# The first feed-forward matrix by seven block products per pair of weight chunks, with half-width matmuls

## The chip, the cores and the metric

One core of one Trainium2 chip runs the whole program. The metric is the device time of one execution in microseconds, as the median over several executions; lower is better. The engines named below are TensorE (PE in the rows, its weight loads PEld), VectorE (DVE), ScalarE (ACT), GpSimd (POOL) and SyncE (SP, which here only starts transfers).

## The reference, cut to what matters

A one-layer decoder trunk on 512 tokens with model width 1024: a mixer (attention and a state-space branch, merged by gates and projected by `w_out`), and then a feed-forward block. All inputs are fp32. The change touches the end of it:

```
h = h + hybrid_mixer(rmsnorm(h, norm1_w), ...)       # its last step: merged @ w_out
gate, up = split(rmsnorm(h, norm2_w) @ w_ffn_in, 2)   # 1024 -> 2 x 2816
h = h + (silu(gate) * up) @ w_ffn_out                 # 2816 -> 1024
return rmsnorm(h, final_norm_w)
```

## The kernel before, in words

**Layout.** Activations lie transposed: 128 features on the partitions, 512 tokens along the row. Every weight matrix is cut into chunks of 128 output features by 1024 (or 512, 768) input features, 512 KB each, and a chunk lies as eight 128x128 tiles side by side.

**Precision.** An fp32 operand is split into a high part, rounded by a copy into the fp32r type, and a low part, the remainder. A product takes three matmuls per 128x128 tile: high times high, high times low, low times high. For weights, class `Weights` (L43) does it for one running list of all chunks: SP loads a raw chunk (L63, tile `wraw`), ScalarE copies the high part (L79, `whi`), VectorE subtracts it from the raw chunk for the low part (L80, `wlo`). It loads two chunks ahead of use and splits one ahead. `project` (L159) takes the next chunk and issues its 24 matmuls of 512 columns (line L104), in one PSUM bank, and at its middle and end runs functions that wait in the list `late` (the norm's steps, for example).

**The stages around the change.** The output projection (L839 to L857) runs eight `project` calls; each result is added to the residual x and gives one 128-feature block `h1` (L843). ScalarE and VectorE split it, scaled by `norm2_w`, into `h1h` and `h1l` (L848, L849), and its squares are summed over blocks by GpSimd (L857). The first feed-forward stage (L870 to L884) has 22 pairs of chunks, gate and up: 2 x 24 matmuls for each pair. The norm's factor per token, `rb2`, is worked out beside the first chunks (`second_norm`, L865) and is multiplied onto gate and up as they leave PSUM (L875, L879); then a tanh (L877), two products on VectorE (L880, L881), and the result `us` is split at once (L179, L180, tiles `hhh`, `hhl`). The second feed-forward stage (L886 to L899) runs, for each of seven output blocks, 22 tiles x 3 matmuls of 512 columns, adds to the residual (L891), squares and scales. The eighth block is written out by hand (`last_block`, L907, and `last_norm`, L919) in two halves of 256 tokens, so 66 matmuls of 256 columns for each half, and the final norm of the first half runs beside the second.

**What sets the order.** Outside the two sections ordered by hand (the start, and the eighth block), a planner orders the instructions of each engine: by their order in the program and by when it expects their inputs. Each engine then runs its list in order. Tiles are taken from pools with a fixed number of buffers per name; a new tile waits until the last reader of the one whose buffer it takes is done. SP, ACT and POOL each start transfers from their own list, so a start waits behind whatever stands before it there.

Of the kernel before, what the change touches and what calls it, by code (L numbers as in the profile page):

```python
# [14 lines left out]
P = 128  # L15
# [11 lines left out]
WARM = 10  # L27

# [63 lines left out]

@with_exitstack
def trunk(ctx: ExitStack, tc: tile.TileContext, xT, w_in, w_v, w_dt, w_attn, w_ssm, w_out, w_fi, w_fo,
# [37 lines left out]
    wst = Weights(nc, wp, _chunk_plan(w_in, w_v, w_attn, w_ssm, w_out, w_fi, w_fo))  # L132
# [26 lines left out]
    def project(ps, rhs, first=True, last=True, at=None):  # L159
        h, l, kt = wst.next()  # L160
# [89 lines left out]
    la_d = drm.tile([NSH, S], F32, name="la_d")  # L250
    v_d = [drm.tile([P, NCH, S], F32, name=f"v_d{g}") for g in range(2)]
# [583 lines left out]
    hp_ = ctx.enter_context(tc.tile_pool(name="h1", bufs=1, reuse_waits="tile", side="right"))  # L835
    h1, h1w = [], []
    h1a = hp_.tile([P, KD, S], F32, name="h1a")
    ssq = None
    for j in range(KD):  # L839
        t = h1a[:, j, :]  # L840
# [4 lines left out]
        h1.append(t)  # L845
        hi = hp_.tile([P, S], F32R, name=f"h1h{j}")
        lo = hp_.tile([P, S], F32R, name=f"h1l{j}")
        act.activation(hi, t, AF.Copy, scale=par("n2", j))  # L848
        ev.scalar_tensor_tensor(lo, t, par("n2", j), hi.bitcast(F32), op0=ALU.mult, op1=ALU.subtract)  # L849
        h1w.append((hi, lo))  # L850
        sq = hp_.tile([P, S], F32, tag="sq", name=f"sq2_{j}", bufs=2)
        act.activation(sq, t, AF.Square)
        if j == 0:
            ssq = hp_.tile([P, S], F32, tag="ssq", name="ssq2")
            gp.tensor_copy(ssq, sq)
        else:
            gp.tensor_add(ssq, ssq, sq)  # L857
    mg_cm.__exit__(None, None, None)
# [4 lines left out]
    rb2 = fp.tile([P, S], F32, name="rb2")  # L863

    def second_norm():  # L865
        r = mean_pow(fp, [ssq], D, EPS, "n2")
        late.append(lambda: act.activation(rb2, spread(r), AF.Copy))

    late.append(second_norm)
    pend = [project(bank("mm"), h1w), project(bank("mm"), h1w)]  # L870
    hh = []
    for j in range(NF):
        pg, pu = pend
        gs = fp.tile([P, S], F32, tag="gs", name=f"gs{j}", bufs=2)
        ev.tensor_mul(gs, pg, rb2)  # L875
        th = fp.tile([P, S], F32, tag="fth", name=f"fth{j}", bufs=2)
        act.activation(th, gs, AF.Tanh, scale=0.5)  # L877
        us = fp.tile([P, S], F32, tag="us", name=f"us{j}", bufs=2)
# [77 lines left out]
def _chunk_plan(w_in, w_v, w_attn, w_ssm, w_out, w_fi, w_fo):  # L956
# [16 lines left out]
    for j in range(NF):  # L973
        plan += [w_fi[j], w_fi[NF + j]]
# [87 lines left out]
```

## Time and profile before

| | us |
|---|---|
| median of 3 runs | 1175.6 (1175.52 to 1177.36) |
| the profiled execution | 1176.68 |
| its span, first to last instruction | 1174.8 |
| output projection | 755.55 to 799.12 |
| first feed-forward stage | 799.12 to 1042.21 |
| second feed-forward stage, blocks 0 to 6 | 1042.21 to 1147.95 |
| eighth block | 1147.95 to the end |

The bounds are the starts of the first matmuls with the stage's operands in the profile's timeline. Times in the rows count from the span's start. A matmul's duration in the rows holds its fill and drain, so neighbouring matmuls overlap; what one costs in a stream is the distance between two starts.

### The profile page before, as it was taken

How to read it: one execution, taken by the hardware profiler on the slowest of the kernel's cores; microseconds unless marked ns; L12 is line 12 of the kernel's file. 1: busy time of each engine (PE TensorE's matmuls, PEld its weight loads, DVE VectorE, ACT ScalarE, POOL GpSimd, SP SyncE). 2: the span in 40 equal slices, each digit the busy share in tenths (PEclk: the TensorE clock that was granted, in tenths of full speed). 3: DMA queues.
4: the chain of work that ended last, by engine and by line, in shares of the span. 5: the costliest groups of instructions: out<-in, count | busy, mean ns of one | idle time of the engine just before them, and what ended most of it. 6: DMA issues, size and time to landing. Idle time of an engine off the chain costs nothing.

```text
span 1174.8 us, 14966 instructions
## 1 busy us (share of the span) xinstructions
PE 1162.8 (99%) x5844; PEld 960.6 (82%) x5844; DVE 632.8 (54%) x1045; ACT 473.6 (40%) x822; POOL 156.3 (13%) x136
## 2 busy tenths in 40 slices
PE   9999999999999999999999999999999999999997
PEld 6777888878888988888888888888888888888886
DVE  5787898874577423456555434454554554532222
ACT  5555465553454321354654533343322322322221
POOL 2214313131112200010110100031000000000001
PEclk9999999999999999999999999999999999999999
DMA  5442323233222343232332213433223333233322
GB/s 211 138 156 92 107 90 116 100 115 102 90 88 75 127 161 106 90 91 82 83 75 88 64 64 99 172 120 93 90 90 108 90 91 107 90 86 94 99 81 72
DMA packets 40584, 120.20 MB, mean 102 GB/s; under 512 B 5368, under 2 KB 11024, under 8 KB 40129
## 3 DMA queue, kind: packets, MB, share of 16 engines
q1 hardware_dynamic: 38224, 116.71, 31.3%
q10 hardware_dynamic: 1296, 2.22, 0.5%
q0 software_dynamic: 992, 0.31, 0.3%
q8 instruction: 46, 0.75, 0.2%
q14 instruction: 26, 0.20, 0.1%
HBM read 114.88 MB, written 4.34 MB: 101 GB/s over the span
## 4 chain that ended last, share of the span: by engine, by line
PE 94%; DVE 2%; issue 1%; DMA 1%; ACT 1%; POOL 0%; SPq 0%; DVEq 0%; ACTq 0%; POOLq 0%
PE mm L104 85%; PE aux L104 7%; PE aux L107 2%; DVE xm L378 0%; DVE wlo L80 0%; DMA x<-xT 0%; DMA la_d<-laf 0%; DMA lab<-la_d 0%; DVE a L470 0%; DVE acc L442 0%; ACT whi L79 0%; ACT xnh L382 0%; DVE xul L301 0%; DVE h1a L941 0%; DVE a L472 0%
## 5 line engine op out<-in xcount | busy, mean ns | idle before, releaser
L79 ACT ACTIVATE whi<-wraw 128x1024 fp32r<-128x1024 f32 (+2 forms) x193 | 198.4, 1028 | 463.1 <-PE mm L104 358.7
L80 DVE TENSOR_TENSOR wlo<-wraw,whi 128x1024 fp32r<-128x1024 f32 (+2 forms) x193 | 238.8, 1238 | 221.8 <-ACT whi L79 221.8
L104 PE MATMUL mm<-xnh,wlo 128*128 128x512 f32 x640 | 254.6, 398 | 0.0
L104 PE MATMUL mm<-xnh,whi 128*128 128x512 f32 x640 | 253.1, 395 | 0.9 <-DVE acc L442 0.8
L104 PE MATMUL mm<-xnl,whi 128*128 128x512 f32 x640 | 252.4, 394 | 0.0
L104 PEld LDWEIGHTS mm<-xnh,wlo 128*128 128x128 f32 x640 | 120.4, 188 | 27.7 <-issue 2.7
L104 PEld LDWEIGHTS mm<-xnh,whi 128*128 128x128 f32 x640 | 120.4, 188 | 27.5 <-issue 1.6
L104 PEld LDWEIGHTS mm<-xnl,whi 128*128 128x128 f32 x640 | 120.3, 188 | 26.6 <-issue 1.2
L104 PE MATMUL mm<-h1h,wlo 128*128 128x512 f32 x352 | 138.8, 394 | 0.0
L104 PE MATMUL mm<-h1l,whi 128*128 128x512 f32 x352 | 138.0, 392 | 0.0
L104 PE MATMUL mm<-h1h,whi 128*128 128x512 f32 x352 | 136.7, 388 | 0.0
L104 PEld LDWEIGHTS mm<-h1l,whi 128*128 128x128 f32 x352 | 66.1, 188 | 15.4
L104 PEld LDWEIGHTS mm<-h1h,whi 128*128 128x128 f32 x352 | 66.1, 188 | 14.7
L104 PEld LDWEIGHTS mm<-h1h,wlo 128*128 128x128 f32 x352 | 66.2, 188 | 13.2
L104 PE MATMUL mm<-hhh,wlo 128*128 128x512 f32 (+1 forms) x198 | 72.9, 368 | 0.0
L104 PE MATMUL mm<-hhl,whi 128*128 128x512 f32 (+1 forms) x198 | 72.6, 367 | 0.0
L104 PE MATMUL mm<-hhh,whi 128*128 128x512 f32 (+1 forms) x198 | 72.4, 365 | 0.0
L442 DVE SCALAR_TENSOR_TENSOR acc<-mm,hcw,acc 128x511 f32<-128x511 f32 (+2 forms) x72 | 53.2, 743 | 1.2 <-ACT acc L440 0.2
L475 POOL TENSOR_TENSOR ce<-ce,Cf 128x768 f32<-128x768 f32 x16 | 34.8, 2177 | 139.4 <-ACT ce L474 78.6
L104 PE MATMUL mm<-ssmh,wlo 128*128 128x512 f32 x128 | 50.6, 395 | 0.0
L104 PE MATMUL mm<-ssml,whi 128*128 128x512 f32 x128 | 50.5, 395 | 0.0
L104 PE MATMUL mm<-ssmh,whi 128*128 128x512 f32 x128 | 49.8, 389 | 0.0
(256 smaller groups left out, 1646.6 us busy)
## 6 DMA issues: line engine op xcount, KB each, us to landing
wraw<-w_in SPq DMA_DIRECT2D x80, 512.0 KB, 3.5
wraw<-w_fi SPq DMA_DIRECT2D x44, 512.0 KB, 3.5
lab<-la_d SPq DMA_DIRECT2D x16, 512.0 KB, 3.7
wraw<-w_ssm SPq DMA_DIRECT2D x16, 512.0 KB, 3.6
wraw<-w_fo SPq DMA_DIRECT2D x16, 512.0 KB, 3.5
wraw<-w_v SPq DMA_DIRECT2D x11, 512.0 KB, 3.5
wraw<-w_out SPq DMA_DIRECT2D x8, 512.0 KB, 3.5
wraw<-w_fo SPq DMA_DIRECT2D x8, 384.0 KB, 3.1
```

Source lines behind the costliest of these rows:

```text
L79: self.nc.scalar.activation(hi[:, cs], r[:, cs], AF.Copy)
L80: self.nc.vector.tensor_sub(lo[:, cs], r[:, cs], hi[:, cs])
L104: pe.matmul(out, lhsT, rhs, start=start, stop=stop, skip_group_check=True)
L107: pe.transpose(out, src, ident)
L442: ev.scalar_tensor_tensor(acc[:, d:], ps[:, : S - d], hcw[:, t * 4 + 3 - d : t * 4 + 4 - d], acc[:, d:], op0=ALU.mult, op1=ALU.add)
L475: gp.tensor_mul(ce, ce, Cf[:, P:].unsqueeze(1).to_broadcast([P, 2, S - P]))
```

## The change

The first feed-forward stage no longer multiplies each chunk with all eight blocks of `h1`. A pair of chunks is seen as a 2x2 matrix of blocks (gate and up, by the first and the last four tiles), the normalised input as a 2x2 matrix too (first and last four feature blocks, by first and last 256 tokens). Their four result blocks come from seven block products instead of eight, over sums and differences of the blocks (Winograd's form of Strassen's scheme). Each product has 4 tiles x 3 matmuls of 256 columns.

- The right-hand sums are made once, in the output projection, whose blocks now come in the order 0, 4, 1, 5, 2, 6, 3, 7 (`OUT_ORDER`); the residual `h1` is written to DRAM there and read back for the second stage.
- For every pair, class `Pairs` loads both raw chunks; the four left-hand sums are added on VectorE and split as before; the three blocks used as they are (a11 and a12 in one piece, a22) get their low part otherwise: ScalarE writes the high part, then its negative into the low part's tile, and a transfer issued by GpSimd adds the raw weights from DRAM onto it.
- Partial sums are copied out of PSUM by ScalarE and added by VectorE. The factor `rb2` is multiplied onto the gate alone; for the up half it is multiplied in the second stage (`rb2h`).
- The first two `us` are split at once (`EARLY`), the other 20 after the stage. The second stage begins with blocks 0 and 1 in turn, eight tiles at a time.

```diff
+class Pairs:
+    def parts(self, pool, tag, name):
+        return tuple(pool.tile([P, KD * P], F32R, tag=tag % n, name=f"{name}_{n}", bufs=3) for n in ("hi", "lo"))
+    def load(self, n):
...
+        r1 = self.wp.tile([P, KD * P], F32, tag="wraw", name=f"fa{n}")
+        r2 = self.fw.tile([P, KD * P], F32, tag="wraw2", name=f"fb{n}", bufs=2)
+        for t, src in ((r2, b), (r1, a)):
+            self.nc.sync.dma_start(t.rearrange("p (k n) -> p k n", n=P), src)
+    def added(self, hi, lo, raw, src):
+        act.activation(hi, raw, AF.Copy)
+        act.activation(lo, hi.bitcast(F32), AF.Copy, scale=-1.0)
+        self.nc.gpsimd.dma_start(lo.rearrange("p (k n) -> p k n", n=P), src, accum_op=ALU.add)
+    def first(self, n):
+        hi, lo = self.parts(self.wp, "w%s", f"fA{n}")
+        self.added(hi, lo, self.raw[n][0], self.pairs[n][0])
...
+    def split(self, n, t, names, key):
+        hi, lo = self.parts(self.fw, "s%s", f"{key}{n}")
+        self.nc.scalar.activation(hi, t, AF.Copy)
+        self.nc.vector.tensor_sub(lo, t, hi)
...
+    def sums13(self, n):
+        self.nc.vector.tensor_add(t[:, :S], r2[:, :S], r2[:, S:])
+        self.nc.vector.tensor_add(t[:, S:], r2[:, :S], r1[:, :S])
+        self.split(n, t, ("s1", "s3"), "fS13")
+    def sums24(self, n):
+        self.nc.vector.tensor_add(t[:, :S], self.sums.pop(n)[:, :S], r1[:, :S])
+        self.nc.vector.tensor_add(t[:, S:], r1[:, S:], t[:, :S])
+        self.split(n, t, ("s2", "s4"), "fS24")
+    def last(self, n):
+        hi, lo = self.parts(self.wp, "w%s", f"fD{n}")
+        self.added(hi[:, :S], lo[:, :S], self.raw.pop(n)[1][:, S:], self.pairs[n][1][:, 4:8])
...
+    for i, j in enumerate(OUT_ORDER):
         ps = project(bank("mm"), merged)
         ev.scalar_tensor_tensor(t, ps, 0.5, t, op0=ALU.mult, op1=ALU.add)
+        nc.sync.dma_start(h1_d[:, j, :], t)
+        if j < 4:
+            act.activation(ff[:, B11 :: B12 - B11, :], tv, AF.Copy, scale=par("n2", j))
+            ev.tensor_sub(ff[:, T1, :], ff[:, B11, :], ff[:, B12, :])
+            rights(p, ff, slice(B11, T1 + 1))
+        else:
+            act.activation(ff[:, B22 : B21 + 1 : B21 - B22, :][:, ::-1, :], tv, AF.Copy, scale=par("n2", j))
+            ev.tensor_sub(ff[:, T3, :], ff[:, B22, :], ff[:, B12, :])
+            ev.scalar_tensor_tensor(ff[:, T2, :], ff[:, B22, :], -1.0, ff[:, T1, :], op0=ALU.mult, op1=ALU.subtract)
+            ev.scalar_tensor_tensor(ff[:, T4, :], ff[:, T2, :], -1.0, ff[:, B21, :], op0=ALU.mult, op1=ALU.subtract)
+            rights(p, ff, slice(B22, T4 + 1))   # high part on ScalarE, low part on VectorE
...
+    def product(ps, n, name, x, first, last):
+        h, l = fi.left[n, name]
+        for p in range(4):
+            xh, xl = right[p][0][:, x, :], right[p][1][:, x, :]
+            k = slice(p * P, p * P + P)
+            mm(ps, h[:, k], xh, start=first and p == 0, stop=False)
+            mm(ps, h[:, k], xl, start=False, stop=False)
+            mm(ps, l[:, k], xh, start=False, stop=last and p == 3)
...
+    for n in range(NF):
+        r = bank("mm")[:, :HS]
+        q, s_ = bank()[:, :HS], bank()[:, :HS]
+        product(r, n, "a11", B11, True, False)
+        c1 = copied(r, "c1", n)
+        fi.first(n + 1)
+        product(q, n, "s1", T1, True, False)
+        c5 = copied(q, "c5", n)
+        fi.last(n)
+        product(s_, n, "a12", B21, True, True)
+        ev.tensor_add(g[:, half[0]], s_, c1)
+        fi.sums13(n + 1)
+        product(r, n, "s2", T2, False, False)
+        u2 = copied(r, "u2", n)
+        if before:
+            finish(*before)      # product(r, n, "a22", T4, False, True); us[:, half[0]] = r * g[:, half[0]]
+        product(q, n, "s4", B22, False, True)
+        ev.tensor_add(g[:, half[1]], q, u2)
+        fi.load(n + 2)
+        fi.sums24(n + 1)
+        ev.tensor_mul(g, g, rb2)
+        act.activation(th, g, AF.Tanh, scale=0.5)
+        product(r, n, "s3", T3, False, False)
+        ev.tensor_add(us[:, half[1]], r, c5)
+        ev.scalar_tensor_tensor(g, th, 1.0, g, op0=ALU.add, op1=ALU.mult)
+        ev.tensor_mul(us[:, half[1]], us[:, half[1]], g[:, half[1]])
...
+    for n in range(EARLY, NF):
+        hh[n] = split(hp_, hraw[n], "hh", n)
...
         t = h1[j]
-        ev.scalar_tensor_tensor(t, ps, 0.5, t, op0=ALU.mult, op1=ALU.add)
+        ev.tensor_mul(add, ps, rb2h)
+        ev.tensor_add(t, t, add)      # in last_norm too
```

## Rows read from the trace of the kernel before

**Rows 1.** The page, parts 1, 2 and 4: engines, granted clock, the last chain.
```profile
PE 1162.8 (99%) x5844; PEld 960.6 (82%) x5844; DVE 632.8 (54%) x1045; ACT 473.6 (40%) x822; POOL 156.3 (13%) x136
PEclk9999999999999999999999999999999999999999
PE 94%; DVE 2%; issue 1%; DMA 1%; ACT 1%; POOL 0%; SPq 0%; DVEq 0%; ACTq 0%; POOLq 0%
```

**Rows 2.** Busy time by stage: engines, clock, DMA share, GB/s.
```profile
799.12:1042.21 243.09, 243.09 (x1070) 199.59 (x1068) 123.56 (x154) 73.16 (x90) 2.84 (x2) 1.00 0.31 95
1147.95:1165.40 17.45, 17.35 (x149) 17.14 (x147) 4.39 (x11) 2.98 (x5) 3.44 (x4) 1.00 0.18 60
```

**Rows 3.** Chain of waits, 740 to 830: start, us, what.
```profile
807.31 0.84 PE aux L104 x8
815.09 0.44 PE aux L107 x4
```

**Rows 4.** Timeline of PE in the eighth block: start, duration, line, tiles.
```profile
1147.95 0.28 PE L104 MATMUL mm<-hhh,whi 128*128 128x256 f32 x1
1151.58 0.28 PE L104 MATMUL mm<-hhh,wlo 128*128 128x256 f32 x1
1152.26 0.28 PE L104 MATMUL mm<-hhl,whi 128*128 128x256 f32 x1
1157.68 0.28 PE L104 MATMUL mm<-hhh,wlo 128*128 128x256 f32 x1
```

**Rows 5.** Groups by shape, 790 to 1075: count, busy, mean ns, idle before and releaser.
```profile
L80 DVE TENSOR_TENSOR wlo<-wraw,whi 128x1024 fp32r<-128x1024 f32 x50 | 61.1, 1223 | 30.1 <-ACT whi L79 30.1
L79 ACT ACTIVATE whi<-wraw 128x1024 fp32r<-128x1024 f32 x49 | 52.0, 1061 | 168.5 <-PE mm L104 98.4 <-issue 70.1
L180 DVE TENSOR_TENSOR hhl<-us,hhh 128x512 fp32r<-128x512 f32 x22 | 15.1, 685 | 2.2 <-ACT hhh L179 2.2
L179 ACT ACTIVATE hhh<-us 128x512 fp32r<-128x512 f32 x22 | 13.9, 633 | 16.5 <-DVE us L881 16.5
L877 ACT ACTIVATE fth<-gs 128x512 f32<-128x512 f32 x22 | 13.5, 616 | 0.0
L848 ACT ACTIVATE h1h<-h1a,prm 128x512 fp32r<-128x512 f32 x2 | 1.4, 714 | 0.0
L843 DVE SCALAR_TENSOR_TENSOR h1a<-mm,h1a 128x512 f32<-128x512 f32 x2 | 1.4, 692 | 5.4 <-PE mm L104 5.4
```

**Rows 6.** Timeline of DVE early in the first stage; idle before it in brackets.
```profile
816.19 0.69 DVE L875 TENSOR_TENSOR gs<-mm,rb 128x512 f32<-128x512 f32 x1 [2.82 <-ACT rb L867]
816.80 0.68 DVE L879 TENSOR_TENSOR us<-mm,rb 128x512 f32<-128x512 f32 x1
818.05 1.23 DVE L80 TENSOR_TENSOR wlo<-wraw,whi 128x1024 fp32r<-128x1024 f32 x1
819.19 1.29 DVE L880 SCALAR_TENSOR_TENSOR gs<-fth,gs 128x512 f32<-128x512 f32 x2
823.58 1.23 DVE L80 TENSOR_TENSOR wlo<-wraw,whi 128x1024 fp32r<-128x1024 f32 x1 [0.22 <-ACT whi L79]
```

**Rows 7.** Groups by shape in the last 85 us: operations on 256 columns.
```profile
L923 DVE SCALAR_TENSOR_TENSOR h1a<-mm,h1a 128x256 f32<-128x256 f32 x2 | 0.8, 424 | 9.2 <-PE mm L104 9.2
L932 ACT ACTIVATE rb<-aux 128x256 f32<-128x256 f32 x2 | 0.8, 385 | 6.0 <-PE aux L107 6.0
```

**Rows 8.** The page, part 6: transfers, KB each, us from issue to landing.
```profile
wraw<-w_fi SPq DMA_DIRECT2D x44, 512.0 KB, 3.5
la_d<-laf POOLq DMA_DIRECT2D x1, 64.0 KB, 4.1
```

**Rows 9.** Groups on POOL, whole span: issues of transfers.
```profile
L670 POOL DMA_DIRECT2D mscr<-m x4 | 3.2, 791 | 103.7 <-DVE m L741 103.7
L692 POOL DMA_DIRECT2D dscr<-d x4 | 2.2, 546 | 2.3 <-ACT L L691 2.2
```

**Rows 10.** Chain of waits at the end: start, us, what.
```profile
1165.34 0.44 DVE h1a L923
```

More of the change, by code (lines that the diff above doesn't have):

```diff
@@ L863, in trunk, with rows @@
     rb2 = fp.tile([P, S], F32, name="rb2")
+    rb2h = fp.tile([P, S], F32, name="rb2h")
+    half = [slice(0, HS), slice(HS, S)]
     def second_norm():
         r = mean_pow(fp, [ssq], D, EPS, "n2")
-        late.append(lambda: act.activation(rb2, spread(r), AF.Copy))
-    late.append(second_norm)
[L870 to L878, printed above, removed]
-        ev.tensor_mul(us, pu, rb2)
-        ev.scalar_tensor_tensor(gs, th, 1.0, gs, op0=ALU.add, op1=ALU.mult)
-        ev.tensor_mul(us, us, gs)
-        hh.append(split(fp, us, "hh", j))
-        if j + 1 < NF:
-            pend = [project(bank("mm"), h1w), project(bank("mm"), h1w)]
+        def rows():
+            pb = spread(r)
+            act.activation(rb2, pb, AF.Copy)
+            act.activation(rb2h, pb, AF.Copy, scale=-0.5)
+        late.append(rows)
@@ new lines, in product, with copied @@
+    def product(ps, n, name, x, first, last):
[6 more added lines that the diff above has]
+            mm(ps, l[:, k], xh, start=False, stop=last and p == 3)
+        now = late[:]
+        del late[:]
+        for f in now:
+            f()
+    def copied(ps, tag, n):
+        t = fp.tile([P, HS], F32, tag=tag, name=f"{tag}_{n}", bufs=2)
+        act.activation(t, ps, AF.Copy)
+        return t
@@ new lines, in trunk @@
+    out_w = Weights(nc, wp, _out_plan(w_fo))
+    out_w.fill(0)
+    finish(*before)
+    fw_cm.__exit__(None, None, None)
+    fr_cm.__exit__(None, None, None)
+    hp_ = ctx.enter_context(tc.tile_pool(name="ho", bufs=1, reuse_waits="tile", side="right"))
+    for n in range(EARLY, NF):
+        hh[n] = split(hp_, hraw[n], "hh", n)
+    h1a = hp_.tile([P, KD, S], F32, name="h1a")
+    h1 = [h1a[:, j, :] for j in range(KD)]
+    for j in range(KD):
+        nc.scalar.dma_start(h1[j], h1_d[:, j, :])
@@ L885, in trunk @@
     ssq = None
+    sums = [bank("mm") for _ in range(2)]
+    for k0 in range(0, NF, 8):
+        for j in range(2):
+            project(sums[j], hh[k0 : k0 + 8], first=(k0 == 0), last=(k0 + 8 >= NF), w=out_w)
     for j in range(KD - 1):
-        ps = bank("mm")
-        for k0 in range(0, NF, 8):
-            project(ps, hh[k0 : k0 + 8], first=(k0 == 0), last=(k0 + 8 >= NF))
+        if j < 2:
+            ps = sums[j]
+        else:
+            ps = bank("mm")
+            for k0 in range(0, NF, 8):
+                project(ps, hh[k0 : k0 + 8], first=(k0 == 0), last=(k0 + 8 >= NF), w=out_w)
@@ L902, in trunk @@
     j = KD - 1
-    HS = S // 2
-    parts = [wst.next() for _ in range(0, NF, 8)]
+    parts = [out_w.next() for _ in range(0, NF, 8)]
     out_v = outT.rearrange("(j p) t -> p j t", p=P)
```

121 lines of the change are left out of this document (92 added, 29 removed).

## The prediction

> **What bounds the kernel now.** I read the page first: the busy line, the row of the granted clock and the chain that ended last. TensorE is busy 99% of the span, its clock stands at full speed (2.4 GHz) in every slice, and 94% of the chain is PE [rows 1]. A busy PE alone proves little, so next I read busy time by stage. In the first feed-forward stage PE is busy in 243.09 of 243.09 us, VectorE in 123.56, ScalarE in 73.16, and the 16 DMA engines 0.31 of the time at 95 GB/s [rows 2]. Nothing but the stream of matmuls sets this stage's length, so it gets shorter only by columns streamed, and longer only if another engine stops keeping up.
>
> The stage holds 2 x 22 x 24 = 1056 matmuls of 512 columns. The chain names 0.84 + 0.44 us in it that are the norm's [rows 3]; the rest is 241.8 us, so one matmul costs 241.8 / 1056 = 0.2290 us and a pair of chunks 48 x 0.2290 = 10.99 us.
>
> What a matmul of 256 columns costs is in the eighth block, which has the same weights, types and three-matmul pattern. The starts 1147.95 and 1151.58 lie 32 matmuls apart: 0.1134 us each. Those at 1152.26 and 1157.68, after a short interruption, lie 46 apart: 0.1178 us each [rows 4]. So half the columns cost 0.495 to 0.514 of the full matmul. There is little to spare: weight loads are in flight for 17.14 of the block's 17.45 us, against 199.59 of 243.09 in the first stage [rows 2].
>
> **The change, part by part.**
>
> *Products.* Before, 1056 matmuls, 241.8 us. After, 22 pairs x 7 products x 12 = 1848 matmuls of 256 columns: 1848 x 0.1178 = 217.7 us, or 1848 x 0.1134 = 209.6 us. I take 0.1178, since it holds for the larger part of the block and came after an interruption, and here every product opens another PSUM bank. That is -24.1 us; the other end is -32.2. A pair then takes 84 x 0.1178 = 9.90 us, and everything else has to fit into that.
>
> *VectorE in a pair.* Back to back, an operation on 512 columns starts the next 0.61 us later (816.19, 816.80) and one on 1024 after 1.14 (818.05, 819.19) [rows 6]; one on 256 columns out of PSUM takes 0.42 [rows 7]. Four sums of 512: 2.4. Two subtractions of 1024: 2.3. Two full-width operations on the gate: 1.2. Five half-width ones: 2.1. Together 8.0 us of 9.90. If all 13 also waited 0.22 us, as the subtraction does behind ScalarE [rows 6], it would be 10.9, so the cost lies between 0 and 1.0 us per pair. I take 0.1 per pair, 2 us in all: the lower end is nearer, because most of these inputs are ready long before use (the sums are made for the next pair).
>
> *ScalarE in a pair.* Four copies of 1024 at 1.06, two of 512 at 0.63, the tanh at 0.62 [rows 5], three copies of 256 out of PSUM at 0.39 [rows 7]: 7.3 us of 9.90. Nothing, while no copy stands behind one that waits. One does wait: the high part of a22 takes the buffer of the piece with a11 and a12 and cannot be written before the third product ends, 36 x 0.1178 = 4.2 us into the pair. Behind it stand the copy of the next partial sum, needed only a product later, and the splits of sums; a22 itself is used in the following pair.
>
> *Transfers.* SP still issues 44 loads of 512 KB. New are 44 issues on POOL (22 of 512 KB, 22 of 256 KB, adding), eight writes of `h1` on SP in the output projection and eight reads on ScalarE's queue in the second stage. The writes wait for VectorE's result and hold up the weight loads queued behind them by that wait only; these run two chunks ahead, and the reads have the second stage's first 30 us (three runs of two chunks) to land. I cost both at nothing. At 95 GB/s for 0.31 busy, the engines would move 306 GB/s [rows 2]: plain loads of 1.05 MB per pair are 3.4 us of work, the added 0.79 MB 2.6 us if adding costs what a copy costs. 6.0 of 9.90 us fits.
>
> *When the low part of a11 lands.* This is the one new wait that PE meets every pair, and every later matmul is queued behind it. In the pair before, the first partial sum is copied by 12 x 0.1178 + 0.39 = 1.8 us; high part and negative take 2 x 1.06, to 3.9; POOL takes up to 0.8 to issue [rows 9], to 4.7; a plain 512 KB lands 3.5 us after its issue [rows 8]: 8.2, against 9.90. The trace has no adding transfer. The nearest rows are that load (3.5 us) and a software-queue transfer of 64 KB (4.1 us) [rows 8]; below, the bound is 0 cost. Above, it lands 3.5 + 1.7 (its data moved twice) + 3.4 (all of the next pair's loads ahead of it) = 8.6 us after issue, at 13.3 us, so 3.4 us late per pair. I take 0, nearest to the 3.5 us row, and keep the other end for a rival.
>
> The Trainium skill speaks against this: "Collectives: The Full Stack", section "The bandwidth ceiling: the fold count and why AG ≠ RS ≠ AR", says that an adding transfer runs at half a copy's rate, because it reads two sources. No run here shows it. By it alone the DMA work of a pair would be about 8.6 us, an estimate, and the sum would not change; what hangs on it is the third rival.
>
> *Into the stage.* After the last output-projection matmul, block 7 must pass: residual 0.69 [rows 5], scaled copy 0.71 [rows 5], three differences of 0.42 [rows 7], high part of 1280 columns (1.06 + 0.63 / 2 = 1.4), low part (1.22 + 0.69 / 2 = 1.6) [rows 5]: 6.0 us. Ready without it are two products and three quarters of the third, 33 x 0.1178 = 3.9 us; and, if the planner draws them forward, three quarters of s2 and s4, another 2.1. So 0 to 2.1 us; I take +1.0. The norm's steps pass PE as before.
>
> *Into the second stage.* Twenty splits of 0.63 and 0.69 [rows 5] that were spread over the first stage now start when the right-hand tiles come free, during the last product. PE eats a tile every 3 x 0.229 = 0.69 us and starts with two that are ready, so it needs the third 1.4 us in, when that is just being finished (0.63 + 0.69 plus a wait); VectorE's pace is 0.61 a tile, plus one weight subtraction per eight tiles, and each group of eight is used for two output blocks. 0 to 4 us; I take +1.0.
>
> *The tail.* In the last half block one operation (0.44 on the chain [rows 10]) becomes two: +0.4. Elsewhere in the second stage the second operation has 15 us of PE beside it.
>
> *Sum*, against the profiled execution of 1176.7 us: -24.1 + 2.0 + 1.0 + 1.0 + 0.4 = -19.7, so 1157.0. The median of the runs lies 1.1 below that execution: **1155.9, forecast 1156**.
>
> **The rivals.**
>
> 1. *The shorter distance holds.* If the products stream at 0.1134 us, 8 us more is gained: 1148. For it: 32 matmuls in a row did. Against: 46 did not.
>
> 2. *Half eaten by VectorE.* Each operation waits a little on PE or ScalarE, the pair takes some 10.4 us, and 22 x 0.5 = 11 us go, less the 2 already counted: 1165. Up to the full 1.0 per pair it would be 1176, no change. For it: 8.0 of 9.90 us, 13 operations in a fixed order, several of them out of banks that PE needs again. Against: nine of the 13 are the sums made a pair ahead and the hidden activations used a stage later, so their lateness need not reach PE.
>
> 3. *The adding transfer is late: slower than before.* Place: the third matmul of each tile of product a11, first in every pair. Price: with twice the data and half of the loads' 3.4 us ahead of it, it lands 3.5 + 1.7 + 1.7 = 6.9 us after issue, at 11.6 us of a pair of 9.90: 1.7 us late, 22 x 1.7 = +37, 1193. It decides from 19.7 / 22 = 0.9 us late per pair, a landing 6.1 us after issue. For it: the next pair's loads start in just this stretch, when a22's copy frees their buffer, and lateness in one pair doesn't free the next, since those loads then come later too. Against: 8 of the product's 12 matmuls need no low part, so if the planner counts with a slow transfer it has other matmuls to put first; and a longer pair gives the loads more time before the next one.
>
> That the saved products don't appear is excluded: their count is in the code.
>
> **How the numbers follow.** Forecast with little stall (1150 to 1161): 0.52. Rival 1 (below 1150): 0.06. Rival 2 (1161 to 1173): 0.12. No change, by either wait: 0.05. Rival 3: 0.25, half of it above 1186. A measurement of this kernel can tell 0.2%, 2.4 us. So faster 0.70, same 0.05, slower 0.25. The range 1146 to 1186 leaves out some 0.15; the likeliest case's own range is 1150 to 1161.
>
> **What would show it.** The first stage should be some 22 us shorter, its 256-column matmuls 0.118 us apart within a product. The chain should stay on PE; if it names the adding transfer or GpSimd's queue ahead of a11, rival 3 holds and issue to landing will read over 6 us; if it names VectorE, rival 2. VectorE should read about 0.8 busy in the stage, ScalarE 0.75, the DMA share 0.6 (0.85 if adding costs twice). A gap of over 3 us at either end of the stage would make those two terms wrong, and matmuls over 0.125 us apart inside a product the whole sum.

## The result and the profile after

The changed kernel takes 1166.06 us (median of 7 runs, 1163.61 to 1171.27), the kernel before 1175.6 (7 runs): ratio 0.9918, 95% interval 0.9898 to 0.9937. It is 9.5 us faster. The sign was right and the time lies in the range, but of the 19.6 us forecast less than half came. The profiled execution takes 1166.95 us, its span 1165.2. The medians of the experiments leave out one execution, of e8, that took 5461 us.

First the page of the changed kernel: the busy line (us, share of the span, instructions), the granted clock in 40 slices, and the shares of the chain that ended last.

```profile
PE 1142.3 (98%) x6636; PEld 981.7 (84%) x6636; DVE 714.2 (61%) x1231; ACT 572.7 (49%) x992; POOL 199.3 (17%) x180
PEclk9999999999999999999999999998999999999998
PE 88%; DVE 5%; DMA 3%; issue 2%; ACT 1%; POOL 0%; SPq 0%; DVEq 0%; ACTq 0%; POOLq 0%
```

Against [rows 1], the chain has lost 6 points on PE, to VectorE and DMA, and the clock has one slice under 9 inside. Where that is, the busy time by stage tells: the whole first stage, its undisturbed middle, the eighth block, and the stretch 779 to 794, in the last blocks of the output projection. As in [rows 2], a row gives the stretch, its length, the busy time and number of instructions of PE, PEld, DVE, ACT and POOL in turn, the granted clock, the DMA share and GB/s.

```profile
798.02:1029.05 231.03, 224.59 (x1873) 223.06 (x1871) 174.67 (x294) 153.62 (x232) 40.67 (x46) 0.99 0.76 174
852.00:1019.40 167.40, 167.40 (x1428) 167.40 (x1427) 131.40 (x220) 115.88 (x170) 29.25 (x34) 1.00 0.81 184
1136.34:1153.84 17.50, 17.00 (x144) 16.79 (x143) 5.36 (x12) 2.98 (x5) 3.44 (x4) 1.00 0.15 48
779.00:794.00 15.00, 15.00 (x68) 12.43 (x67) 15.00 (x21) 10.51 (x14) 8.94 (x4) 1.00 0.53 182
```

The last of these stretches in the kernel before:

```profile
779.00:794.00 15.00, 15.00 (x68) 12.43 (x67) 6.60 (x9) 5.28 (x9) 5.37 (x3) 1.00 0.32 107
```

In the middle PE is busy in 167.40 of 167.40 us: nothing reaches it there. The stage's idle time, 6.4 us, lies near its start: 5.8 us of it ahead of 826 and 0.6 from there to 850. And in 779 to 794, ahead of the stage, VectorE has no free time left (15.00 of 15.00, from 6.60).

The pitch in the middle, on PE's timeline (start, duration): the same matmul of the same pattern, two pairs apart.

```profile
881.64 0.28 PE L175 MATMUL mm<-frh,fS_hi 128*128 128x256 f32 x1
901.38 0.28 PE L175 MATMUL mm<-frh,fS_hi 128*128 128x256 f32 x1
```

19.74 us for 168 matmuls: 0.1175 us each, 9.87 a pair, close to the 0.1178 of the later rows of the eighth block [rows 4].

Now PE at the start of the stage.

```profile
798.14 0.28 PE L175 MATMUL mm<-frl,fA_hi 128*128 128x256 f32 x1
800.06 0.36 PE L175 MATMUL mm<-frh,fA_lo 128*128 128x256 f32 x1 [1.63 <-DMA fA_lo<-w_fi]
801.42 0.39 PE L175 MATMUL mm<-frh,fA_hi 128*128 128x256 f32 x1
805.93 0.58 PE L175 MATMUL mm<-frh,fA_lo 128*128 128x256 f32 x1 [4.12 <-DMA fA_lo<-w_fi]
808.44 0.41 PE L175 MATMUL mm<-frh,fA_lo 128*128 128x256 f32 x1
```

The first wait is for the low part of pair 0, the second for that of pair 1, whose product the planner had drawn forward. Between 798.02 and 810.22 lie 24 matmuls of the products (2.8 us at 0.1175) and the norm's eight small ones (about 1 us): some 8.4 of these 12.2 us are lost, to the two waits, smaller gaps and a slower clock together. The clock falls during the second wait: from 803.4 to 810.2 the granted clock is 0.50, that is 1.2 GHz, and a matmul takes 0.21 us instead of 0.12.

```profile
803.40:810.20 6.80, 4.27 (x20) 4.28 (x21) 4.84 (x6) 2.29 (x4) 1.25 (x1) 0.50 0.54 154
```

Who is late is on three more timelines of the same 25 us: GpSimd, ScalarE's queue (one load), VectorE.

```profile
786.51 5.97 POOL L951 TENSOR_TENSOR ssq<-ssq,sq 128x512 f32<-128x512 f32 x1 [5.69 <-DVE s L143]
792.43 0.92 POOL L121 DMA_DIRECT2D fA_lo<-w_fi  x1
793.37 1.50 POOL L951 TENSOR_TENSOR ssq<-ssq,sq 128x512 f32<-128x512 f32 x1
798.23 0.88 POOL L121 DMA_DIRECT2D fA_lo<-w_fi  x1 [3.36 <-ACT fA_lo L120]
```
```profile
795.81 0.33 ACTq L927 DMA_DIRECT2D h<-xT  x1
```
```profile
793.29 0.41 DVE L941 TENSOR_TENSOR ff<-ff 128x256 f32<-128x256 f32 x1
793.63 1.51 DVE L942 SCALAR_TENSOR_TENSOR ff<-ff 128x256 f32<-128x256 f32 x1
802.07 0.69 DVE L929 SCALAR_TENSOR_TENSOR h<-mm,h 128x512 f32<-128x512 f32 x1 [1.36 <-DMA h<-xT]
807.93 1.49 DVE L921 TENSOR_TENSOR frl<-ff,frh 128x1280 fp32r<-128x1280 f32 x1
```

Four things go wrong together. GpSimd's running sum of squares takes 5.97 us instead of 1.3 to 1.6, and the first adding transfer, ready since 790.2, is issued behind it. It lands 7.6 us after that. Beside the next sum (793.37 + 1.50), a difference on VectorE that takes 0.41 a moment before takes 1.51. And the load of the last block's x, issued at 795.81 because a tile came free late, holds VectorE's residual until 802.07, so that the last right-hand tile ends at 809.4, 11.4 us after the projection's end (798.02).

At the start of the second stage:

```profile
1030.76 0.73 PE L175 MATMUL mm<-hhh,whi 128*128 128x512 f32 x2 [1.55 <-ACT hhh L250]
1032.10 0.79 PE L175 MATMUL mm<-hhl,whi 128*128 128x512 f32 x1 [0.61 <-DVE hhl L251]
1032.69 0.63 PE L175 MATMUL mm<-hhh,wlo 128*128 128x512 f32 x1
```

Two waits (1.71 and 0.88 us, counted from where the stream would have gone on), and 3.4 us at 1.2 GHz, from 1032.1 to 1035.5. The planner had put the 12 matmuls on the two hidden tiles that were ready ahead of the last product, where no wait was, and they were missing here.

### The profile page after: what moved, and what is told of

Read it like the earlier page. It is cut to its first block, busy times and chain, and to the rows that moved or that the text cites. A ratio compares the mean times of both kernels' runs of the same rounds, so it can differ in the third digit from the quotient of the medians.

```text
span 1165.2 us, 17113 instructions
## 1 busy us (share of the span) xinstructions
PE 1142.3 (98%) x6636; PEld 981.7 (84%) x6636; DVE 714.2 (61%) x1231; ACT 572.7 (49%) x992; POOL 199.3 (17%) x180
## 4 chain that ended last, share of the span: by engine, by line
PE 88%; DVE 5%; DMA 3%; issue 2%; ACT 1%; POOL 0%; SPq 0%; DVEq 0%; ACTq 0%; POOLq 0%
PE mm L175 71%; PE aux L175 15%; PE aux L178 2%; DMA fb<-w_fi 1%; DVE wlo L82 1%; DMA fA_lo<-w_fi 1%; DVE xm L450 0%; ACT whi L81 0%; DMA x<-xT 0%; DMA la_d<-laf 0%; DMA lab<-la_d 0%; DVE ff L942 0%; DVE a L542 0%; DVE fS_lo L134 0%; DVE acc L514 0%
## 5 line engine op out<-in xcount | busy, mean ns | idle before, releaser
L82 DVE TENSOR_TENSOR wlo<-wraw,whi 128x1024 fp32r<-128x1024 f32 (+2 forms) x156 | 185.4, 1193 | 193.1 <-ACT whi L81 193.1
L81 ACT ACTIVATE whi<-wraw 128x1024 fp32r<-128x1024 f32 (+2 forms) x156 | 152.2, 981 | 283.2 <-PE mm L175 252.7
L175 PE MATMUL mm<-hhh,whi 128*128 128x512 f32 (+1 forms) x180 | 66.8, 372 | 1.6 <-ACT hhh L250 1.6
L175 PE MATMUL mm<-hhh,wlo 128*128 128x512 f32 (+1 forms) x180 | 66.0, 368 | 0.0
L134 DVE TENSOR_TENSOR fS_lo<-s,fS_hi 128x1024 fp32r<-128x1024 f32 x44 | 52.9, 1216 | 0.7 <-ACT fS_hi L133 0.7
L175 PE MATMUL aux<-frh,fS_hi 128*128 128x256 f32 x176 | 50.0, 284 | 0.5 <-ACT fS_hi L133 0.5
L175 PE MATMUL mm<-frh,fS_lo 128*128 128x256 f32 x176 | 49.8, 283 | 0.0
L175 PE MATMUL aux<-frh,fS_lo 128*128 128x256 f32 x176 | 49.8, 283 | 0.0
L175 PE MATMUL aux<-frl,fS_hi 128*128 128x256 f32 x176 | 49.8, 283 | 0.0
L175 PE MATMUL mm<-frl,fS_hi 128*128 128x256 f32 x176 | 49.8, 283 | 0.0
```

What stands on the lines that cost most here:

```text
L81: self.nc.scalar.activation(hi[:, cs], r[:, cs], AF.Copy)
L82: self.nc.vector.tensor_sub(lo[:, cs], r[:, cs], hi[:, cs])
L134: self.nc.vector.tensor_sub(lo, t, hi)
L175: pe.matmul(out, lhsT, rhs, start=start, stop=stop, skip_group_check=True)
```

## The experiments

Each run is of the changed kernel with the edits named. The program ahead of the output projection is the same in all of them, but the projection's start varies between 753.6 and 758.9 us in the profiles. So besides the median the table has the stretch from that start to the first matmul of the eighth block in the profile, which holds all that the change touches but the tail; it was 392.40 before. It is one execution of each run, and it also moves with things that no edit named here sets, of 1.6 and 2 us (the clock and the matmuls' pitch in the second stage, below).

| run | edits | median us | ratio to before [95%] | stretch us |
|---|---|---|---|---|
| changed kernel | | 1166.06 | 0.9918 [0.9898, 0.9937] | 381.88 |
| e1 | subtract in pairs 0, 1 | 1164.39 | 0.9902 [0.9884, 0.9920] | 378.70 |
| e2 | third residual buffer | 1167.57 | 0.9931 [0.9904, 0.9958] | 381.51 |
| e3 | squares on TensorE, 64 columns | 1167.06 | 0.9935 [0.9917, 0.9953] | 381.00 |
| e4 | subtract in all pairs | 1165.41 | 0.9913 [0.9894, 0.9931] | 378.97 |
| e5 | e1 + e2 | 1165.04 | 0.9906 [0.9890, 0.9922] | 381.03 |
| e6 | squares on VectorE | 1170.64 | 0.9952 [0.9936, 0.9969] | 383.90 |
| e7 | second stage's tiles placed | 1165.63 | 0.9910 [0.9895, 0.9925] | 378.50 |
| e8 | e6 + e7 | 1168.29 | 0.9937 [0.9920, 0.9953] | 383.09 |
| e9 | pair 0 early | 1167.32 | 0.9935 [0.9919, 0.9952] | 380.83 |
| e10 | e9 + e2 | 1166.84 | 0.9931 [0.9916, 0.9946] | 381.73 |
| e11 | e7 + order written out | 1165.25 | 0.9913 [0.9897, 0.9929] | 379.21 |
| e12 | e10 + e11 | 1164.79 | 0.9908 [0.9893, 0.9924] | 379.64 |
| e13 | squares on TensorE by ones | 1166.19 | 0.9913 [0.9896, 0.9929] | 379.46 |
| e16 | e13 + e2 + e11 | 1161.32 | 0.9879 [0.9860, 0.9899] | 373.85 |
| e14 | e16 + e1 | 1157.87 | 0.9850 [0.9833, 0.9866] | 372.02 |
| e18 | e14 without e11 | 1158.18 | 0.9852 [0.9835, 0.9868] | 374.95 |
| e15 | e16 + e9, subtract in pair 1 | 1156.85 | 0.9841 [0.9826, 0.9855] | 371.99 |
| e17 | e15 without e13 | 1163.59 | 0.9900 [0.9885, 0.9915] | 377.18 |

The third residual buffer is paid for, wherever it stands, with one of the squares' two buffers.

**First round: one link at a time.** Low parts by subtraction (e1 with SUB = 2, e4 with 99), the buffer (e2), the sums of squares on TensorE (e3):

```diff
+        if n < SUB:
+            self.nc.vector.tensor_sub(lo, raw, hi)
+            return
```
```diff
-        t = tmp.tile([P, S], F32, tag="t", name=f"h1_{j}", bufs=2)
+        t = tmp.tile([P, S], F32, tag="t", name=f"h1_{j}", bufs=3)
...
-        sq = tmp.tile([P, S], F32, tag="sq", name=f"sq2_{j}", bufs=2)
+        sq = tmp.tile([P, S], F32, tag="sq", name=f"sq2_{j}", bufs=1)
```
```diff
-            gp.tensor_add(ssq, ssq, sq)
+        square_sums(ssq, sq, i == 0, i == KD - 1)   # 4 matmuls of 64 columns into a bank
```

> The changed kernel, but for pairs 0 and 1 the low parts of a11, a12 and a22 come from a VectorE subtraction, as all low parts did before the change; the other 20 pairs keep the adding transfer. Theory A (the adding transfers of the first two pairs land late, 7.7 us after issue, and PE stands for them 1.6 and 4.1 us at the start of the first stage): both waits go, and with them the half-speed clock behind them; 6 to 8 us less than the changed kernel's 1166, so 1158 to 1160. Theory B (the last blocks of the output projection reach the right-hand sums late, because the residual's x is loaded late into one of two buffers; the transfer is only what PE happened to name): PE waits for the right-hand operands instead, at most 2 us are saved, 1164 to 1166. Theory C (GpSimd's sums of squares and VectorE hold each other up during the output projection): VectorE is yet busier by 2 x 1.9 us there, 1166 or more.

> The changed kernel with three instead of two buffers for the residual blocks of the output projection (and one instead of two for their squares), so that x is loaded a block earlier. Theory A: PE still waits for the adding transfers, within 2 us of 1166. Theory B: the last residual sum starts at about 798.8 instead of 802.07, the right-hand operands are there 3 us earlier and the start of the stage gets 3 to 6 us shorter, 1160 to 1163. Theory C: within 2 us of 1166.

> The changed kernel with the sums of squares of the output projection taken from GpSimd: TensorE adds them up instead, four matmuls of 64 columns for each of the eight blocks, some 0.4 us each, 2.7 us more on PE. GpSimd then has only the adding transfers. Theory C: VectorE's 256-column operations fall from up to 1.5 us to 0.42, it has 5 us less to do before the stage, the first adding transfers are issued at once, and the start gets 6 to 9 us shorter; less 2.7 for PE, 1160 to 1163. Theory A: the first transfer is issued 2.3 us earlier (at 790.2 instead of 792.4), the second one no earlier; 1164 to 1168. Theory B: 1166 to 1169.

> The changed kernel with no adding transfer at all: all low parts by VectorE subtraction. In the steady part VectorE is now busy 131.4 us in 17 pairs, 7.7 us of 9.85 per pair; 1.2 + 0.6 more makes 9.5 of 9.85. If the adding transfers are what lets the pairs run at 9.85 us, PE waits for VectorE and a pair takes 10.2 us or more, 22 x 0.35 = 8 us: 1166 to 1175 even with the start of e1. If they are not needed, the pairs stay at 9.85 us and the time is that of e1 within 2 us, and the DMA share falls from 0.81 to about 0.35.

In e1, as its theory B said, the transfers are gone and PE waits as long for another operand, as its waits show (PE, line, what it waited for, us in total, times, longest):

```profile
PE mm L179 <- ACT frh L924: 4.5, 1, 4.5
PE mm L179 <- DVE frl L925: 0.5, 1, 0.5
```

e4's answer has the same 4.5 us, so the adding transfers alone are not the cause. e4 settles another question: in its stretch 860 to 1000 PE is busy all 140.00 us with VectorE at 133.52 and DMA at 0.33. The adding transfer is not needed for the pace, nor does it harm it. e2 alone gives nothing, so a late load of x (its theory B) is not the cause by itself: its waits are for fA_lo, 6.3 us in three. In e3, as theory C said, the start is nearly clear:

```profile
PE mm L175 <- DMA fA_lo<-w_fi: 0.9, 1, 0.9
PE mm L175 <- DVE frl L921: 0.7, 1, 0.7
```

and the first stage 6.4 us shorter, but the output projection 49.12 us instead of 43.56: the six groups of 64-column matmuls that lie in it cost 5.6 us, 0.93 a group where 0.34 had been expected (2.7 for eight), and the time stayed.

**Second round: pairs of links, GpSimd, the second stage.** e6 adds up the squares on VectorE; e7 gives hidden tiles 2 to 11 the place of the sums of weights, which are free earlier, and the others that of the right-hand tiles.

```diff
-            gp.tensor_add(ssq, ssq, sq)
+            ev.tensor_add(ssq, ssq, sq)
```
```diff
+    late_h = {n: tuple(hp_.tile([P, S], F32R, name=f"hh{x}{n}") for x in "hl") for n in (*range(12, NF), *range(EARLY, 12))}
```

> Both edits together that alone moved nothing: the low parts of the first two pairs by subtraction on VectorE (no adding transfer there), and three residual buffers, so that the last block's x is loaded a block earlier. Theory 1 (two chains of equal length end at the stage's start; the right-hand one is late because of its load of x): with both cut the wait of 4.6 us for the right-hand tile goes down to under 1.5 us, half a clock with it, and the time falls from 1166 to 1158 to 1161 us. Theory 2 (VectorE and GpSimd hold each other up in the last blocks, and that alone makes the right-hand chain late): the load comes earlier, the 256-column operations of VectorE still take about 1.5 us instead of 0.42, the wait stays over 3 us and the time at 1163 to 1166 us.

> The running sum of the squares of the second norm on VectorE instead of GpSimd; adding transfers and buffers as in the changed kernel. Theory 2 (the two engines hold each other up): VectorE's 256-column operations go back from 1.5 us to about 0.42, GpSimd is free when the first low part is ready, so that the adding transfer is issued some 1.5 us earlier, VectorE takes 8 x 0.69 = 5.5 us more work but stays under the stage's length; the waits of the first pair fall from 8.4 us to 2 to 3 us, the half clock goes, and the time falls to 1157 to 1161 us. Rival (VectorE is then the bound of the output projection's last blocks): the right-hand tiles come 3 us or more late, the time stays at 1164 to 1167 us.

> Only the places of the second stage's split tiles are changed: the ten that are needed first lie over the sums of weights, which are free before the last product, and the hidden blocks 12 to 21 and the residual over the right-hand tiles. Theory (the second stage waits because its first splits can't begin until the last product is done): the waits of 1.7 and 0.9 us and the half clock of 3.4 us (some 1.7 us of loss) go, and the time falls by 3 to 4.3 us to 1162 to 1163 us. Rival (the splits come earlier but stand on ScalarE and VectorE before the last pair's own work, which makes the last product late): no gain, 1165 to 1167 us.

> The sums of squares on VectorE and the new places together. If the two losses (start of the first stage, start of the second) are apart, the gains add: 1166 minus 5 to 9 minus 3 to 4.3, 1153 to 1158 us, near the forecast of 1156. If one of them falls, the time is that of the other edit alone.

e5 keeps e1's 4.5 us for the right-hand tile. Its load of x now comes early, but VectorE takes up the last residual only at 802.91, behind other work. e6 is slower than the changed kernel. VectorE's 256-column operations are back at 0.42 us, as expected, but the engine was full and has 5.5 us more, and ScalarE, whose queue also issues the load of x, stood for 5.97 us behind that load until a tile came free. The transfer came after that, and e8, with the same sums, waits 9.1 us for it:

```profile
809.64 0.55 PE L175 MATMUL mm<-frh,fA_lo 128*128 128x256 f32 x1 [8.61 <-DMA fA_lo<-w_fi]
```

e7 leaves the waits of the second stage's start as they were (1.71 and 0.88 us). Its clock stayed up there, but not by its edit: in e1, e4, e5 and e9, whose second stage is untouched, the same waits have no half clock behind them either. From the matmul that ends the first of these waits to the eighth block e1, e4, e7 and e9 take 104.0 us and the changed kernel 105.6, so the half clock is worth 1.6 us. The rest of e7's shorter stretch lies in the start of the first stage, which its edit does not touch (waits of 2.3 and 1.6 us there). The reason for the second stage's waits is on ScalarE's timeline of the changed kernel; in e7 the row is the same, at 1029.07: a split of weights waits for the last product to free its buffer, and the hidden tiles' splits stand behind it in order.

```profile
1029.13 1.06 ACT L81 ACTIVATE whi<-wraw 128x1024 fp32r<-128x1024 f32 x1 [2.91 <-PE mm L175]
1030.10 4.77 ACT L250 ACTIVATE hhh<-us 128x512 fp32r<-128x512 f32 x9
```

**Third round: VectorE's full stretch, and ScalarE's order.** e9 moves pair 0's left parts and the loads of pair 1 three blocks up; e11 adds a written order to e7.

```diff
-        if i == KD - 3:
+        if i == 2:
             fi.load(0)
-        if i == KD - 2:
+        if i == 3:
             fi.first(0)
```
```diff
+    out_w.fill(1)
+    fixed = tc.manual_schedule(engines={mybir.EngineType.Activation, mybir.EngineType.DVE})
...
+        if n == 7:
+            out_w.fill(2)
+            fixed.__exit__(None, None, None)
```

> The loads, the left-hand sums, the splits and the first adding transfer of pair 0, and the loads of pair 1, are moved from the last two blocks of the output projection up to its third and fourth, where VectorE has idle time (it is busy for 15.0 of 15 us at 779 to 794 in the changed kernel, against 6.6 before). Theory 3 (VectorE is full in these 15 us, so that everything behind it, right-hand tiles and left-hand parts alike, comes late): the transfer of pair 0 has landed long before the stage, VectorE keeps only the right-hand chain in the last blocks, the waits at the start fall from 8.4 to 2 to 4 us, and the time to 1157 to 1161 us. Rival (the last block's x, whose load waits for a buffer, holds ScalarE and the right-hand tiles anyway): waits of 4 us and more for the right-hand tiles, 1163 to 1166 us.

> The same with three residual buffers, so that ScalarE's queue doesn't stand behind the load of the last block's x. By theory 3 with the load of x as a second link: the right-hand tiles of the last block come 2 to 3 us after the projection's end at most, no half clock, 1155 to 1158 us. If the load is no link: the same as without the third buffer.

> The second stage's start: the new places of the split tiles, and ScalarE's and VectorE's order written out there, so that the splits of hidden blocks 2 to 7 stand ahead of the weight split that waits for the last product to free its buffer. With the places alone the wait of 1.71 us stayed, because that weight split stood first on ScalarE. Theory: the waits of 1.71 and 0.88 us and the half clock go; the stretch from the first matmul of the first stage to that of the eighth block falls by 3.5 to 4.5 us, the time to 1161.5 to 1163 us. Rival (ScalarE's next operation, not its order, is late): the waits stay, 1165 to 1167 us.

> Pair 0 early, three residual buffers and the second stage's new places and order together. If the two starts are the whole of what the forecast missed: 1151 to 1155 us, below the forecast of 1156 and the changed kernel's 1166. If the gains of the two overlap or go into another wait: 1156 to 1161 us.

e11 did to the waits what was expected: ScalarE begins the six splits at 1028.49 and the weight split comes after them.

```profile
1028.49 3.24 ACT L1059 ACTIVATE hhh<-us 128x512 fp32r<-128x512 f32 x6 [2.32 <-PE mm L175]
1031.63 1.05 ACT L81 ACTIVATE whi<-wraw 128x1024 fp32r<-128x1024 f32 x1
```

The 1.71 us wait and the half clock are gone. The stretch is 2.7 us shorter, but only 1.4 of that lies in the second stage (105.91 us against 107.29); the rest is in the start of the first. The median, 0.8 lower, does not show a gain outside its uncertainty. In the second stage something else eats a part: in e5, e11 and e12 its 512-column matmuls stand 0.2333 us apart, at the same granted clock, and 0.229 in the kernel before and in all other runs, some 2.0 us over the seven blocks. 60 us of it in e11 and then in e14, which has e11's edit too (259 and 264 matmuls):

```profile
1050.00:1110.00 60.00, 60.00 (x259) 48.61 (x258) 19.92 (x22) 18.92 (x23) 5.97 (x5) 1.00 0.33 97
1050.00:1110.00 60.00, 60.00 (x264) 49.24 (x263) 18.64 (x20) 17.31 (x20) 5.17 (x4) 1.00 0.33 97
```

The cause is not known: e5 leaves the second stage as it was, and e14 to e17 have e11's edit at the usual pitch and take 103.9 us for it. e9, e10 and e12 missed their theories' times: pair 0 was there in time, and PE stood 3.2 to 3.8 us for the low part of pair 1, which the planner puts ahead of the rest of pair 0, and 0.9 to 1.0 for a right-hand tile. Moving work out of VectorE's full stretch is not enough either. A cheaper way to take the sums from GpSimd was still to be tried.

**Fourth round: the sums by ones, then the other links besides.** One 512-column product per block, with a tile of ones on the left, adds the squares up in a bank, with the squares rounded like the other operands:

```diff
-            gp.tensor_add(ssq, ssq, sq)
+        mm(sums2, ones_r, sq, start=(i == 0), stop=(i == KD - 1))
```

> The squares of the second norm are summed on TensorE by one 512-column product per block with a tile of ones (one value rounded as the other operands are), not by GpSimd; nothing else changed. Price by the 512-column pitch of the projection, 0.227 us: 8 x 0.227 = 1.8 us. Theory 4 (one cause, GpSimd's sum): VectorE's 256-column operations at 0.42 us, the stage's waits 2 to 3 us and no half clock as in the run with 64-column sums, and so 1166 - 8 + 1.8 = 1159 to 1161 us. Theory 5 (several chains end together, each edit lays the next one bare): waits of 4 us and more stay for the left part of pair 1 or the right-hand tiles, 1163 to 1167 us.

> The same with three residual buffers, subtraction instead of adding transfers in pairs 0 and 1, and the second stage's places and order. All known chains are cut but VectorE's load in 779 to 794. Theory 4: 1155 to 1158 us (1160 less 2.7 of the second stage, less up to 1 for the chains). Theory 5 with VectorE full as the last link: right-hand tiles 3 us late and more, 1159 to 1163 us.

> Sums of squares by ones on TensorE, pair 0 early, pair 1's low part by subtraction, three residual buffers, second stage as before: nothing late is left but the right-hand chain of the last block itself (some 10 us from the projection's end, of which about 6 are covered by products of pairs 0 and 1). Theory 5: 1154 to 1158 us, the best of all. Theory 4: no better than the run with the sums and the subtraction alone.

> Sums of squares by ones on TensorE, three residual buffers, second stage's places and order; adding transfers as in the changed kernel. Theory 4: 1156 to 1159 us, as with subtraction. Theory 5: the left part of pair 0 or 1 is late by the transfer's 5.6 to 7.7 us, 1159 to 1163 us.

The six products that lie in the projection cost 1.5 us there (it takes 45.05), all eight some 2. In e13 the start's waits fall to 2.5 us for the transfer and 0.7 for the norm, as theory 4 said, but the clock falls after the first of them (0.55), and the stretch is 2.4 us shorter; the median doesn't move, as theory 5 said.

```profile
808.30:811.80 3.50, 3.10 (x13) 2.59 (x13) 1.29 (x2) 0.36 (x1) 0.00 (x0) 0.55 0.55 125
```

e16 still waits 2.0 us for a transfer, with the time that theory 5 gave. e15 has e11's places and order, as in the table, where its expectation says "second stage as before". e14 and e15 have no such wait left; the one line of their waits in 752 to 850 is the norm's own:

```profile
PE aux L179 <- ACT ssq L958: 0.7, 1, 0.7
```

and their stretches are 20.4 us shorter than before's 392.40, with some 2 us for the squares in them. The forecast had -24.1 + 2.0 + 1.0 + 1.0 = -20.1 for them. In part the totals agree by luck: e14's parts are -24.7 for the products, +1.4 and +0.9 for the two starts and +2.0 for the squares, which the forecast did not have, while its +2.0 for VectorE did not come. That the starts then cost about the +1.0 each that was forecast is no luck of this kind.

VectorE is as full in e14 as in the changed kernel, and PE does not wait:

```profile
779.00:794.00 15.00, 15.00 (x67) 12.39 (x66) 14.82 (x21) 10.13 (x13) 0.00 (x0) 1.00 0.52 159
```

So a full VectorE by itself (theory 3) does not make the stage late. e14's last right-hand tile ends 7.8 us after the projection's end, where the changed kernel's came after 11.4.

**Last round: is each link needed?** e17 is e15 with GpSimd's sums; e18 is e14 with the second stage as it was.

> The best kernel so far (1156.9 us) with the sums of squares back on GpSimd, all its other edits kept. If GpSimd's sums hold the right-hand chain up (256-column operations of VectorE at 1.3 to 1.5 us instead of 0.42, two or three of them in the last block's chain), waits of 2 to 4 us return at the first stage's start, against 1.8 us of TensorE saved: 1158 to 1162 us. If the other chains were the whole cause: 1155 to 1156 us, below the best so far by those 1.8 us.

> Sums of squares by ones on TensorE, subtraction in pairs 0 and 1 and three residual buffers, with the second stage's places and order as in the changed kernel. If the losses of the two starts add: 1157.9 + 2.7 to 3.4 = 1160.5 to 1161.5 us, waits of 1.7 and 0.9 us and half a clock at the second stage's start. If the second start's loss is given back later: 1158 us.

e17 loses 6.7 us of time and 5.2 of the stretch. VectorE's last differences, of e17 and then of e15:

```profile
808.65 0.42 DVE L946 SCALAR_TENSOR_TENSOR ff<-ff 128x256 f32<-128x256 f32 x1
809.10 1.37 DVE L947 SCALAR_TENSOR_TENSOR ff<-ff 128x256 f32<-128x256 f32 x1
```
```profile
801.25 0.42 DVE L948 SCALAR_TENSOR_TENSOR ff<-ff 128x256 f32<-128x256 f32 x1
801.70 0.42 DVE L949 SCALAR_TENSOR_TENSOR ff<-ff 128x256 f32<-128x256 f32 x1
```

and e17's longest wait at the start is for the sum itself:

```profile
PE aux L179 <- POOL ssq L955: 2.3, 1, 2.3
```

One of the last block's three differences is slow, by 1 us. The rest of e17's loss lies elsewhere: VectorE takes up the last residual 2.2 us after the projection's last matmul (0.04 in e15), PE waits 0.6 and 1.0 us for split weights inside the projection, and the clock is at 0.50 from 811 to 814, behind the 2.3 us. That the sums must leave GpSimd is shown, since e17 and e15 differ only in them; that the two engines holding each other up is the whole way in which they cost time is not.

So GpSimd's sums are one necessary link: e13 alone, and e15's other edits alone, leave 1166 and 1164. The low parts by subtraction are another: e14 and e16 differ only there, by 3.5 us in the median (the intervals just touch), and e16's 2.0 us wait is what e14 lacks. The third buffer was never taken back by itself, so its share is not shown. e18's stretch is 2.9 us longer than e14's, with the waits of 1.71 and 0.88 us back, but its median is only 0.3 above. What the second start's loss is worth in the time, when the first is clear, stays open; the profiled execution, in which a half clock follows these waits, was the slowest of e18's four.

## Why the prediction was wrong, and where it was right

*Right.* The products: 9.87 us a pair against the 9.90 forecast. *VectorE and ScalarE in a pair*: 0.78 and 0.69 busy against 0.8 and 0.75, and no wait in the middle, so the +2.0 was 0. *Transfers* and *when the low part of a11 lands*: hidden in every pair but the first two, though the DMA share in the middle is 0.81, near the 0.85 that the prediction gave for adding at twice the cost and not its 0.6. Rival 3 thus did not come; its mark, a landing over 6 us, was not reached at the median by the transfers that a11 waits for (5.6, below), and a22's, with 6.6, are used a pair later. In the middle the sum was right, 22 x (10.99 - 9.87) = 24.7 us.

*Wrong: "Into the stage", +1.0, bounds 0 to 2.1.* The first stage without the 12 matmuls of the second that were drawn into it takes 231.03 - 2.75 = 228.28 us. 22 x 9.87 and the norm's 1.28 [rows 3] make 218.4, so its start cost 9.9 us. The step followed one chain, the last block's right-hand side, through durations that each operation has when it runs alone, and saw its inputs as there. It left out three things that the rows of the changed kernel show. The left-hand parts and transfers of pairs 0 and 1 had been costed as pairs that have a pair's time before them; here they begin at the stage's very edge, each with 5.6 to 7.7 us of transfer behind it. The work that I put into the output projection at no cost fills VectorE, from 6.60 to 15.00 of 15.00 us in 779 to 794; by e14 that alone does not make the stage late, but it leaves nothing over for a delay. And two of the engines hold each other up there. The runs show no single culprit: subtraction, the buffer and the sums on TensorE each alone left 1164 to 1168 us, since another chain ends at about the same time (the transfer of pair 1 at 805.9 in the changed kernel, the right-hand tile at 805.4 in e1); with the sums off GpSimd and all others cut, the waits are gone, the start costs 1.4 us by the same count (e14), and the time is near the forecast (1156.85 and 1157.87 against 1156), in part by luck as said above.

*Wrong: "Into the second stage", +1.0, bounds 0 to 4.* From the end of the first stage to the eighth block it was 1136.34 - 1029.05 = 107.29, and 2.75 of its work had been done before: 110.04 against 105.74, so +4.3, of which 1.6 is the half clock. I counted on the two ready tiles as cover for the third; the planner spent them earlier. And I had the splits wait for the right-hand tiles, not behind a weight split on ScalarE. e11's order takes both waits to a total of some 0.8 us, and in e14 the term is +0.9.

*The tail*, +0.4: from the eighth block's first matmul to the norm's last ones it was 20.08 and is 21.44, +1.4, since PE's gap at the last squares is 1.58 us instead of 1.12 and one of 0.66, ahead of GpSimd's sum, is new; to the end of the span it is 26.85 and 28.86, +2.0. No run tests it.

*The sum as measured*: -24.7 + 9.9 + 4.3 + 2.0 = -8.5. The profiled execution's projection also began 1.1 us earlier than before's (754.46, 755.55), which gives the 9.6 us between the spans, 1174.8 and 1165.2.

*Rival 2* (1165) has the time, but not its mechanism: no time was lost in the pairs.

## What to carry to other kernels

A stage that pipelines well in its middle is paid for at its edges: list for its first two iterations every input on every engine, not the one chain that the steady state would suggest, and price the work put ahead of the stage by the durations that it has beside the other engines' work there, not by those that it has alone (0.42 us became 1.4 here). When several chains end together, cutting one shows nothing, and says nothing against it: cut all, then put them back one at a time.

## What the runs showed of the hardware

*Adding transfers.* Between 755 and 1030 the software queue that carries them takes 37.7% of the engines for 17.30 MB, the plain loads' queue 33.1% for 28.71 MB (packets, MB, share; then transfers, KB each, median us from issue to landing):

```profile
q0 software_dynamic: 6336, 17.30, 37.7%
q1 hardware_dynamic: 9504, 28.71, 33.1%
fA_lo<-w_fi POOLq DMA_DIRECT2D x22, 512.0 KB, 5.6
fD_lo<-w_fi POOLq DMA_DIRECT2D x22, 256.0 KB, 6.6
```

That is 2.18% against 1.15% per MB, 1.89 times as much. The page of the Trainium skill that the prediction cites ("Collectives: The Full Stack", section "The bandwidth ceiling: the fold count and why AG ≠ RS ≠ AR") says of the adding steps of a collective, against its copying ones, that they read two sources and run at half the rate; 1.89 is near that. The landings [rows 8] went from 3.5 to 5.6 us for 512 KB, 7.6 in the first two pairs, within the forecast's 3.5 to 8.6.

*VectorE and GpSimd.* In the changed kernel operations of VectorE that start beside a running sum on GpSimd end 0.2 to 0.3 us after it (793.63 + 1.51 against 793.37 + 1.50), at 1.4 to 1.5 us instead of 0.41 to 0.43, and where VectorE runs such operations back to back the sum takes 5.97. With the sums elsewhere (e6, e14, e15) all take 0.42. The Trainium skill has it in "SBUF — State Buffer", section "Who interferes with whom": an elementwise operation with both inputs in that memory contends with GpSimd's reads, and one waits for the whole of the other. The rows agree.

*Small matmuls in a stream.* Six groups of four fp32 matmuls of 64 columns lengthened the projection by 5.6 us (e3), 0.93 a group; six products of 512 columns by 1.5 (e13), 0.25 each.

*The pitch.* In the second stage 512-column matmuls stood 0.2333 us apart in e5, e11 and e12 and 0.229 in all other runs, both at a granted clock of 1.00. No run tells why.

*The clock.* At the first stage's start it fell to 1.2 GHz in the runs whose longest wait was 2.3 us (e7, e17), 2.5 (e13) and 3.2 to 9.1 (the changed kernel, e1, e2, e4 to e6, e8 to e12), and not in e16, whose longest was 2.0. In the second stage the same waits of 1.71 and 0.88 us were followed by half a clock in the changed kernel, e2, e3, e6, e10, e13 and e18, and not in e1, e4, e5, e7, e8 and e9, so a wait's length alone does not tell. There the half clock cost 1.6 us (105.6 us to the eighth block instead of 104.0).
